# Differential attention on one core: one value product per key tile, or one for each of its two softmax maps

## The chip, the cores and the metric

One core of a Trainium2 chip runs the whole program, a hybrid backbone of two layers. The metric is device time in microseconds (us) of one execution, taken as the median of several. The engines are named as the profile names them: PE is TensorE, PEld its weight loads, DVE is VectorE, ACT is ScalarE, POOL is GpSimd, SP issues DMAs.

## The reference

Each layer normalises 256 context and 1024 latent tokens, projects them, mixes them in three head groups (an RWKV-7 scan in two directions, differential attention, windowed grouped-query attention), projects the result and passes it through a gated MLP. The change touches the differential attention alone. It has four heads; each head has two components m with their own queries and keys of width 32 and a shared value of width 64:

```python
def diff_core(q, k, v, lam):
    s = jnp.einsum('bqhmd,bkhmd->bhmqk', q, k, preferred_element_type=F32) * (DF_QK ** -0.5)
    p = jax.nn.softmax(s, axis=-1)
    p = p[:, :, 0] - lam * p[:, :, 1]
    return jnp.einsum('bhqk,bkhd->bqhd', p.astype(v.dtype), v)
...
    head_out = lambda t: (rms_norm(t, norm_g) * (1.0 - lam_init)).reshape(t.shape[:2] + (DF_W,))
```

Context queries see the 256 context keys, latent queries all 1280 keys.

## The kernel before

Per layer, one stage runs three generators side by side: the RWKV scan (`rw_rest` and what it calls), the differential attention (`df_units`) and the modulation vectors (`ada`). When the scan has ended, the windowed attention (`gq_units`) begins beside the last differential units. A scheduler of the framework, which places instructions by a simulated timeline, decides the order on each engine; dependencies and the buffers of each pool bound it. Every engine then works its own list in order.

A unit of differential attention is one head and one group of query blocks: two context blocks (layer 0 only) or four latent blocks, so 12 units in layer 0 and 8 in layer 1. A unit has two halves, which `streams` interleaves with those of other units:

- `scores` (L1341): for each query block, component and chunk of keys, a score product into a bank `ds` (L1363, L1376), the negated row maximum on DVE (L1365, L1378), and an exponential on ACT that sums its row (L1356). The maxima and sums of the chunks are merged (L1386 to L1392). Then `neg_log` (L1294) works out minus the logarithm of the sum on eight DVE instructions and three ACT exponentials that alternate, L1395 adds it to the row maximum, and `max_rows` (L1214) puts the sum into eight extra rows of the queries, by a product into a bank `od` (L1223) and a DVE product (L1224).
- `values` (L1400): for each tile j of 128 keys, the score product of each component, keys on partitions (L1419, 104 rows, the extra rows among them), and an exponential on ACT (L1420), which thus gives normalised weights. DVE forms p0 + (-lambda) p1 (L1425, `p[:, 0]` of a tile `p`, three buffers). The product with the 128x64 values (L1432) accumulates in 64 of the 128 partitions of the bank `od`: even j in 0 to 63, odd j in 64 to 127. Products are put off by a list `late`, two at a time. After the last one, ACT copies the bank to `doT` (L1409); four products with `fold`, two stacked identities (L1412), add the two halves and turn them to token-major form in a `ds` bank; DVE copies that (L1327), and a root-mean-square norm follows (L1329 to L1334).

There is one `od` bank, and two banks for `ds`, `ada` and the output projection together. All operands of the value product are fp32, and each such product appears in the trace as two passes: 168 products, 336 records. One product uses half of the array's columns.

Of the kernel before, what the change touches and what calls it, by code (L numbers as in the profile page):

```python
# [83 lines left out]
PCP = ()  # L84
# [16 lines left out]
LN2 = math.log(2.0)  # L101
# [56 lines left out]
class K:  # L158
# [1044 lines left out]
    DF_TAGS = ("ks", "qs", "p", "vh", "dy", "dsq", "doT", "mask8d", "fold", "dnm", "dL", "dmn", "dtot", "dnl", "lni", "lne", "dss", "drs", "ms",  # L1203
# [90 lines left out]
    def neg_log(self, y, L, n):  # L1294

        v = self.nc.vector
        it = self.al("lni", [128, 8], 2, I32)[:, :n]
        e = self.al("lne", [128, 8], 2)[:, :n]
        v.tensor_copy(y, L.bitcast(I32))
        v.tensor_scalar(out=y, in0=y, scalar1=-LN2 / (1 << 23), scalar2=LN2 * (127 - 0.043), op0=ALU.mult, op1=ALU.add)  # L1300
        for _ in range(3):
            self.nc.scalar.activation(e, y, AF.Exp)
            v.tensor_tensor(out=e, in0=e, in1=L, op=ALU.mult)
            v.scalar_tensor_tensor(out=y, in0=y, scalar=1.0, in1=e, op0=ALU.add, op1=ALU.subtract)

    def df_units(self, l, late):
# [6 lines left out]
        for hd in range(DF_HEADS):  # L1313
# [11 lines left out]
            def finish(o, t0, nt, hd=hd):  # L1325
                y = self.al("dy", [128, 4, 64], 1)[:, :nt]
                vv.tensor_copy(y, o)  # L1327
# [9 lines left out]
            for gi, (t0, nt) in enumerate(groups):  # L1337
# [3 lines left out]
                def scores(t0=t0, nt=nt, nk=nk, us=us, hs=hs, first=gi == 0, head=head, hd=hd):  # L1341
# [51 lines left out]
                    nl = f(self.al("dnl", [128, 2, nt], 3))  # L1393
                    self.neg_log(nl, tot, 2 * nt)
                    vv.tensor_tensor(out=rows, in0=nl, in1=rows, op=ALU.add)  # L1395
# [4 lines left out]
                def values(t0=t0, nt=nt, nk=nk, us=us, hs=hs, finish=finish):  # L1400
# [4 lines left out]
                    pair = []  # L1405

                    def result():
                        s = self.al("doT", [128, 512], 1)[:, :w]
                        act.activation(s, o[:, :w], AF.Copy)  # L1409
                        u = self.bk(UFB)  # L1410
                        for i in range(nt):
                            mm(u[:, i * 64:i * 64 + 64], s[:, i * 128:i * 128 + 128], self.fold, start=True, stop=True)  # L1412
                        finish(u[:, :nt * 64].rearrange("p (t d) -> p t d", t=nt), t0, nt)

                    for j in range(nk):
# [5 lines left out]
                        if j in PCP:  # L1421
                            gp.tensor_scalar(out=p[:, 1, :w], in0=p[:, 1, :w], scalar1=self.nlam, scalar2=None, op0=ALU.mult)
                            gp.tensor_tensor(out=p[:, 0, :w], in0=p[:, 0, :w], in1=p[:, 1, :w], op=ALU.add)
                        else:
# [877 lines left out]
```

## Time and profile before

| what | before |
|---|---|
| median of 3 runs | 4567.54 us (4542.02 to 4578.57) |
| profiled execution | 4560.47 us, span 4558.6 us |
| PE busy | 4169.8 us (91%) |
| DVE busy | 2917.1 us (64%) |
| ACT busy | 1797.8 us (39%) |
| POOL busy | 2180.7 us (48%) |
| mean granted clock of TensorE | 0.892 |

Busy shares are means over stages with different limits. The differential attention runs from about 430 to 1265 us (layer 0) and from about 2880 to 3640 us (layer 1), and only these stretches hold instructions that the change touches. The chain of waits follows the work that ended last back from the end, so a piece of work on it is time that the end waited for. The granted clock has two levels, 1.0 (2.4 GHz) and 0.5 (1.2 GHz); a fraction is a mean over a stretch.

### The profile page before, as it was taken

The page shows a single profiled execution, that of the slowest core. Times are in us where ns is not written, and L with a number is a line of the kernel's source. Part 1 is how long each engine was busy: PE and PEld are TensorE (multiplying, and loading weights), DVE is VectorE, ACT ScalarE, POOL GpSimd, SP SyncE. Part 2 cuts the span into 40 slices and gives each one's busy share as a digit, 9 for nine tenths or more (in the row PEclk, how much of TensorE's full clock was granted, in tenths as well). Part 3 has the DMA queues.
Part 4 walks back from the last instruction along what each step waited for, and adds up shares of the span by engine and source line. Part 5 has one row for each costly group of instructions (what it writes and reads, how often), then busy time and mean ns, then how long its engine had stood idle before and what let it go on. Part 6 is the DMA issues. An engine that isn't in the chain of part 4 may idle for free.

```text
span 4558.6 us, 67583 instructions
## 1 busy us (share of the span) xinstructions
PE 4169.8 (91%) x24447; PEld 3182.7 (70%) x24447; DVE 2917.1 (64%) x5849; ACT 1797.8 (39%) x3586; POOL 2180.7 (48%) x2151
## 2 busy tenths in 40 slices
PE   8998888898998799979998998888989998999898
PEld 5886655665466699968996786645845466788786
DVE  4346676567665877788777336766677656766443
ACT  3334554544323333343333334555534333333332
POOL 3335324334353666666665425264243445766443
PEclk9997778796899899989998998668988988999999
DMA  6454232234023222232223646132241142222443
GB/s 205 137 135 109 62 85 78 69 95 119 27 68 126 93 84 78 81 116 88 79 84 114 166 115 144 43 80 60 59 121 34 29 133 87 79 83 84 146 149 121
DMA packets 465626, 440.44 MB, mean 97 GB/s; under 512 B 122115, under 2 KB 389515, under 8 KB 465292
## 3 DMA queue, kind: packets, MB, share of 16 engines
q1 hardware_dynamic: 408780, 369.39, 27.4%
q0 software_dynamic: 24352, 62.80, 4.9%
q10 hardware_dynamic: 32160, 3.94, 0.5%
q8 instruction: 193, 3.16, 0.3%
q14 instruction: 141, 1.16, 0.1%
HBM read 340.96 MB, written 95.04 MB: 96 GB/s over the span
## 4 chain that ended last, share of the span: by engine, by line
PE 73%; DVE 13%; DMA 5%; ACT 3%; issue 3%; POOL 2%; SPq 1%; ACTq 0%; DVEq 0%; POOLq 0%
PE m L249 6%; PE m L250 6%; PE m L251 6%; PE b L249 3%; PE b L250 3%; PE od L1432 3%; PE b L251 3%; PE gs L1499 2%; PE gram L955 2%; PE dn L249 2%; PE dn L250 2%; PE dn L251 2%; PE ds L1419 2%; PE gs L1498 2%; PE fm L249 2%
## 5 line engine op out<-in xcount | busy, mean ns | idle before, releaser
L245 POOL TENSOR_TENSOR gp<-gx,gp 128x512 fp32r<-128x512 f32 x160 | 208.4, 1307 | 257.3 <-DVE gp L241 181.9
L239 ACT ACTIVATE fwh<-wraw 128x1024 fp32r<-128x1024 f32 x198 | 206.0, 1055 | 273.0 <-DVE wraw L1849 190.8
L1356 ACT ACTIVATE ds<-ds,dnm 128x512 f32<-128x512 f32 (+1 forms) x400 | 232.4, 581 | 189.2 <-DVE dnm L1378 112.4
L1420 ACT ACTIVATE p<-ds 128x512 f32<-128x512 f32 (+1 forms) x336 | 187.2, 585 | 254.8 <-PE ds L1419 211.8
L245 DVE TENSOR_TENSOR wl<-wraw,fwh 128x1024 fp32r<-128x1024 f32 x110 | 196.8, 1790 | 114.0 <-ACT fwh L239 111.8
L245 POOL TENSOR_TENSOR wl<-wraw,fwh 128x1024 fp32r<-128x1024 f32 x88 | 222.4, 2530 | 95.8 <-ACT fwh L239 95.5
L249 PE MATMUL m<-h,fwh 128*128 128x322 f32 (+1 forms) x660 | 219.8, 333 | 11.0 <-ACT fu L1895 6.8
L1378 DVE TENSOR_REDUCE dnm<-ds 128x1 f32<-128x512 f32 x256 | 173.6, 686 | 84.9 <-PE ds L1376 82.2
L251 PE MATMUL m<-h,wl 128*128 128x322 f32 (+1 forms) x660 | 218.8, 332 | 2.9 <-DVE wl L245 2.9
L245 DVE TENSOR_TENSOR wl<-wr,wh 128x512 fp32r<-128x512 f32 (+1 forms) x76 | 66.6, 878 | 241.8 <-ACT wh L239 128.2
L250 PE MATMUL m<-h,fwh 128*128 128x322 f32 (+1 forms) x660 | 220.1, 334 | 0.0
L245 POOL TENSOR_TENSOR wl<-wr,wh 128x512 fp32r<-128x512 f32 (+1 forms) x76 | 99.8, 1313 | 246.8 <-ACT wh L239 208.1
L1425 DVE SCALAR_TENSOR_TENSOR p<-p,ls 128x512 f32<-128x512 f32 (+1 forms) x168 | 144.8, 863 | 95.3 <-ACT p L1420 93.3
L1432 PE MATMUL od<-p,vh 128*64 128x512 f32 (+1 forms) x336 | 191.0, 707 | 13.4 <-DVE p L1425 9.2
L1376 PE MATMUL ds<-ks,qs 96*128 96x512 f32 x256 | 155.5, 625 | 44.5 <-ACT ds L1356 37.5
L250 PE MATMUL dn<-dl,ahl 128*128 128x512 f32 x440 | 177.5, 403 | 4.4 <-POOL dl L245 4.4
L249 PE MATMUL dn<-dh,ahl 128*128 128x512 f32 x440 | 175.3, 402 | 5.2 <-ACT ahl L239 3.8
L245 POOL TENSOR_TENSOR dl<-dr,dh 128x1024 fp32r<-128x1024 f32 x44 | 109.5, 2489 | 143.2 <-ACT dh L239 143.2
L249 PE MATMUL m<-T,fwh 128*128 128x322 f32 (+1 forms) x436 | 147.1, 338 | 32.7 <-DVE fraw L1866 23.7
L251 PE MATMUL dn<-dh,ahl 128*128 128x512 f32 x440 | 171.4, 399 | 0.0
L1419 PE MATMUL ds<-qs,ks 104*128 104x512 f32 (+1 forms) x336 | 152.7, 496 | 8.8 <-ACT p L1420 5.9
L245 DVE TENSOR_TENSOR dd<-dr,dd 128x1024 fp32r<-128x1024 f32 x44 | 59.0, 1344 | 156.9 <-ACT dd L239 156.9
(572 smaller groups left out, 13490.3 us busy)
## 6 DMA issues: line engine op xcount, KB each, us to landing
dr<-in_ff_w_down_dram SPq DMA_DIRECT2D x88, 512.0 KB
aw<-in_ada_w_dram SPq DMA_DIRECT2D x160, 256.0 KB
wraw<-in_ff_w_gate_dram SPq DMA_DIRECT2D x66, 512.0 KB
wraw<-in_ff_w_up_dram SPq DMA_DIRECT2D x66, 512.0 KB
wr<-in_w_in_dram SPq DMA_DIRECT2D x88, 256.0 KB
x<-scr_x SPq DMA_DIRECT2D x28, 512.0 KB
scr_act<-cv POOLq DMA_DIRECT2D x22, 512.0 KB, 3.0
ar<-scr_act SPq DMA_DIRECT2D x44, 256.0 KB
```

The lines of the kernel that those rows point to most:

```text
L239: nc.scalar.activation(hi, src, AF.Copy)
L245: e.tensor_tensor(out=lo, in0=src, in1=hi, op=ALU.subtract)
L249: mm(out, lh, rh, start=first, stop=False)
L250: mm(out, lh, rl, start=False, stop=False)
L251: mm(out, ll, rh, start=False, stop=last)
L1356: act.activation(s, s, AF.Exp, bias=nm[:, c, m, i:i + 1], accum_out=L[:, c, m, i:i + 1])
L1376: mm(s, us["q"][m][0:96, i * 128:i * 128 + 128], K2[m][0:96, 256 + 512 * c:768 + 512 * c], start=True, stop=True)
L1378: vv.tensor_reduce(out=nm[:, 1 + c, m, i:i + 1], in_=s, axis=AX.X, op=ALU.max, negate=True)
L1419: mm(s[:, :w], hs["K"][m][0:104, j * 128:j * 128 + 128], us["q"][m][0:104, :w], start=True, stop=True)
L1420: act.activation(p[:, m, :w], s[:, :w], AF.Exp)
L1425: vv.scalar_tensor_tensor(out=p[:, 0, :w], in0=p[:, 1, :w], scalar=self.nlam, in1=p[:, 0, :w], op0=ALU.mult, op1=ALU.add)
L1432: mm(o[r:r + 64, :w], v[:, j], p[:, 0, :w], start=j < 2, stop=j >= nk - 2)
```

## The change

The weights of the value product are no longer normalised, and the two components are no longer subtracted before it. For each key tile there are now two products with the same values, one for each component: component 1 into partitions 64 to 127 of `od`, component 0 into 0 to 63, the second queued directly behind the first. After the last tile the bank is transposed whole (four 128x128 transposes in place of the four products with `fold`), and a DVE product multiplies each component by the reciprocal of its sum, times -lambda for component 1; POOL adds the two. `neg_log` and `fold` go, and the extra query rows hold the row maximum alone. A list `late` now takes one tile's two products at a time, and the reciprocals have five buffers. The diff, without lines that only drop names:

```diff
-            def finish(o, t0, nt, hd=hd):
+            def finish(u, r, t0, nt, hd=hd):
+
+                t = self.al("doT", [128, 512], 1)[:, :nt * 128].rearrange("p (b m d) -> p b m d", b=nt, m=2)
+                vv.tensor_tensor(out=t, in0=u, in1=r.rearrange("p (m b) -> p b m", m=2).unsqueeze(3).broadcast_to([128, nt, 2, 64]), op=ALU.mult)
                 y = self.al("dy", [128, 4, 64], 1)[:, :nt]
-                vv.tensor_copy(y, o)
+                gp.tensor_tensor(out=y, in0=t[:, :, 0], in1=t[:, :, 1], op=ALU.add)
...
-                    nl = f(self.al("dnl", [128, 2, nt], 3))
-                    self.neg_log(nl, tot, 2 * nt)
-                    vv.tensor_tensor(out=rows, in0=nl, in1=rows, op=ALU.add)
+                    r = us["r"] = f(self.al("dnl", [128, 2, nt], 5))
+                    vv.reciprocal(out=r, in_=tot)
+                    vv.tensor_scalar(out=r[:, nt:], in0=r[:, nt:], scalar1=self.nlam, scalar2=None, op0=ALU.mult)
...
                         for i in range(nt):
-                            mm(u[:, i * 64:i * 64 + 64], s[:, i * 128:i * 128 + 128], self.fold, start=True, stop=True)
-                        finish(u[:, :nt * 64].rearrange("p (t d) -> p t d", t=nt), t0, nt)
+                            nc.tensor.transpose(u[:, i * 128:i * 128 + 128], s[:, i * 128:i * 128 + 128], self.ident)
+                        finish(u[:, :w].rearrange("p (b m d) -> p b m d", b=nt, m=2), us["r"], t0, nt)
...
-                        if j in PCP:
-                            gp.tensor_scalar(out=p[:, 1, :w], in0=p[:, 1, :w], scalar1=self.nlam, scalar2=None, op0=ALU.mult)
-                            gp.tensor_tensor(out=p[:, 0, :w], in0=p[:, 0, :w], in1=p[:, 1, :w], op=ALU.add)
-                        else:
-                            vv.scalar_tensor_tensor(out=p[:, 0, :w], in0=p[:, 1, :w], scalar=self.nlam, in1=p[:, 0, :w], op0=ALU.mult, op1=ALU.add)
-
-                        pair.append((j, p))
-
-                        def product(pair=tuple(pair)):
-                            for j, p in pair:
-                                r = 64 * (j % 2)
-                                mm(o[r:r + 64, :w], v[:, j], p[:, 0, :w], start=j < 2, stop=j >= nk - 2)
+
+                        def product(j=j, p=p):
+
+
+                            i1 = mm(o[64:128, :w], v[:, j], p[:, 1, :w], start=j == 0, stop=j == nk - 1)
+                            with self.tc.issue_after(i1.ins):
+                                mm(o[0:64, :w], v[:, j], p[:, 0, :w], start=j == 0, stop=j == nk - 1)
                             if j == nk - 1:
                                 result()
 
-                        if j % 2:
-                            late.append(product)
-                            pair.clear()
+                        late.append(product)
                         self.flush(late, DLD[l])
```

Three places in the engines' lists show what moves. The first is PE in layer 0, in the first head's second latent unit: `ds` are score products of successive key tiles, `od` the value products, the rest is RWKV. Before:

```order
L1419 MATMUL ds1697_8410<-qs1569_7863,ks1509_7571 128x512
L1419 MATMUL ds1699_8417<-qs1569_7863,ks1509_7571 128x512
L1432 MATMUL od1669_8295<-p1692_8398,vh1510_7574 64x512
L1419 MATMUL ds1700_8420<-qs1569_7863,ks1509_7571 128x512
L1419 MATMUL ds1702_8425<-qs1569_7863,ks1509_7571 128x512
L814 MATMUL wl1074_5247<-lora551_2775,wa1036_5122 128x256 x2
L1432 MATMUL od1669_8295<-p1695_8406,vh1510_7574 64x512
```

The same unit after the change (L1406 is the score product, L1412 and L1414 the two value products):

```order
L1406 MATMUL ds1694_8382<-qs1564_7836,ks1508_7568 128x512
L1406 MATMUL ds1695_8385<-qs1564_7836,ks1508_7568 128x512
L1412 MATMUL od1663_8258<-p1690_8372,vh1509_7571 64x512
L1414 MATMUL od1663_8258<-p1690_8372,vh1509_7571 64x512
L1406 MATMUL ds1697_8391<-qs1564_7836,ks1508_7568 128x512
L882 MATMUL bon1064_5208<-cols548_2769,bs1063_5205 128x2 x2
L1406 MATMUL ds1698_8394<-qs1564_7836,ks1508_7568 128x512
L1412 MATMUL od1663_8258<-p1693_8381,vh1509_7571 64x512
L1414 MATMUL od1663_8258<-p1693_8381,vh1509_7571 64x512
```

Before, the products of the two column halves mostly stand apart, with score products between them; now the two of a tile stand together, one pair for each tile.

The second place is DVE at the end of that unit's `scores` half (L1391 and L1392 merge the sums, L1378 are the next unit's maxima). Before:

```order
L1391 TENSOR_TENSOR dtot1561_7828<-dL1532_7681 128x8
L1392 TENSOR_TENSOR dtot1561_7828<-dtot1561_7828,dL1532_7681 128x8
L773 SCALAR_TENSOR_TENSOR rk1035_5115<-raw1033_5109,pt97_385,rk1035_5115 128x256
L1299 CAST dnl1562_7836<-dtot1561_7828 128x8
L885 COPY bonus557_2787<-bon910_4380 128x4
L773 SCALAR_TENSOR_TENSOR rk1035_5115<-raw1033_5109,pt97_385,rk1035_5115 128x256
L1300 TENSOR_SCALAR dnl1562_7836<-dnl1562_7836 128x8
L1378 TENSOR_REDUCE dnm1570_7865<-ds1575_7883 128x1
L1378 TENSOR_REDUCE dnm1570_7865<-ds1576_7887 128x1
L1303 TENSOR_TENSOR lne1564_7838<-lne1564_7838,dtot1561_7828 128x8
```

After:

```order
L1381 TENSOR_TENSOR dtot1558_7813<-dtot1558_7813,dL1529_7666 128x8
L771 SCALAR_TENSOR_TENSOR rk1035_5115<-raw1033_5109,pt97_385,rk1035_5115 128x256
L883 COPY bonus557_2787<-bon910_4380 128x4
L1222 TENSOR_TENSOR qs1527_7663<-od1561_7827,mask8d1507_7566 8x512
L1383 RECIPROCAL dnl1559_7821<-dtot1558_7813 128x8
L1367 TENSOR_REDUCE dnm1565_7838<-ds1571_7860 128x1
L1384 TENSOR_SCALAR dnl1559_7821<-dnl1559_7821,ls819_4030 128x4
```

The alternation with ACT is gone, and the extra rows (L1222) are written before the sum's reciprocal instead of after the logarithm.

The third place is PE at the end of the unit. Before:

```order
L1432 MATMUL od1669_8295<-p1714_8493,vh1510_7574 64x512
L1419 MATMUL ds1722_8515<-qs1569_7863,ks1509_7571 128x512
L1432 MATMUL od1669_8295<-p1717_8503,vh1510_7574 64x512
L1432 MATMUL od1669_8295<-p1720_8511,vh1510_7574 64x512
L1412 MATMUL ds1724_8525<-fold1508_7568,doT1723_8523 128x64 x4
```

After:

```order
L826 MATMUL kk1080_5269<-ident_87,rx1079_5267 128x128 x2
L1412 MATMUL od1663_8258<-p1715_8477,vh1509_7571 64x512
L1414 MATMUL od1663_8258<-p1715_8477,vh1509_7571 64x512
L834 MATMUL az1050_5163<-wa1036_5122,lora551_2775 128x256
L1399 MATMUL ds1719_8490<-ident_87,doT1718_8488 128x128 x4
```

Four transposes stand where the four products with `fold` stood.

## Rows read from the trace of the kernel before

**Rows 1.** Page, part 4: shares of the chain that ended last, by engine.

```profile
PE 73%; DVE 13%; DMA 5%; ACT 3%; issue 3%; POOL 2%; SPq 1%; ACTq 0%; DVEq 0%; POOLq 0%
```

**Rows 2.** Busy time by stretch, both stages: us, PE, PEld, DVE, ACT, POOL, PEclk.

```profile
430.00:1265.00 835.00, 749.39 (x5708) 474.49 (x5707) 576.04 (x1471) 397.40 (x980) 322.05 (x480) 0.78 0.28 73
2880.00:3640.00 760.00, 697.33 (x5096) 439.71 (x5096) 519.41 (x1251) 366.20 (x883) 316.78 (x457) 0.83 0.24 62
```

**Rows 3.** The DVE subtraction (page, part 5), and who waited for it (us, times).

```profile
L1425 DVE SCALAR_TENSOR_TENSOR p<-p,ls 128x512 f32<-128x512 f32 (+1 forms) x168 | 144.8, 863 | 95.3 <-ACT p L1420 93.3
...
PEld od L1432: 22.2, 34
PE od L1432: 9.2, 11
```

**Rows 4.** Chain of waits, pieces in both stages: start us, us; first and last each.

```profile
581.26 0.04 DVE p L1425
...
3376.43 0.66 DVE p L1425
...
434.06 0.40 DVE lne L1303
...
3537.73 0.08 DVE dmn L1395
...
552.10 0.59 PE ds L1412 x4
...
3628.42 0.97 PE ds L1412 x8
...
548.73 0.58 PE od L1432 x4
...
3626.59 1.00 PE od L1432 x2
```

**Rows 5.** Timeline of value products: start us, us, and records merged (two a product).

```profile
614.09 1.07 PE L1432 MATMUL od<-p,vh 128*64 128x512 f32 x2 [0.47 <-DVE p L1425]
...
3005.57 1.97 PE L1432 MATMUL od<-p,vh 128*64 128x512 f32 x2
...
3356.98 1.98 PE L1432 MATMUL od<-p,vh 128*64 128x512 f32 x4
...
3034.77 2.63 PE L1432 MATMUL od<-p,vh 128*64 128x512 f32 x4 [2.14 <-DVE p L1425]
3035.43 0.29 PEld L1432 LDWEIGHTS od<-p,vh 128*64 128x64 f32 x2 [0.37 <-DVE p L1425]
```

**Rows 6.** Timeline: four fold products; three 128x128 transposes; then one transpose (min/median/max ns).

```profile
588.22 1.00 PE L1412 MATMUL ds<-fold,doT 128*128 128x64 f32 x8
...
39.54 0.55 PE L493 MATMUL hTp<-ident,x 128*128 128x128 f32 x3
...
L493 PE MATMUL hTp<-ident,x x160: 270/273/476, 39.5 to 2643.2; 128*128 128x128 f32 x160
```

**Rows 7.** Groups by form on DVE: one step of the logarithm, and a reciprocal.

```profile
L1303 DVE TENSOR_TENSOR lne<-lne,dtot 128x8 f32<-128x8 f32 x48 | 11.6, 241 | 8.8 <-ACT lne L1302 8.6
...
L1533 DVE RECIPROCAL ges<-ges 128x4 f32<-128x4 f32 x36 | 6.2, 171 | 0.4
```

**Rows 8.** Lines that answer to the new finish (min/median/max ns; the second from stage 1's groups).

```profile
L1327 DVE COPY dy<-ds x20: 291/424/426, 552.7 to 3629.4; 128x256 f32<-128x256 f32 x16, 128x128 f32<-128x128 f32 x4
...
L957 DVE TENSOR_TENSOR G<-gram,gmask 128x512 f32<-128x512 f32 x40 | 27.5, 690 | 12.1 <-PE gram L955 11.1 <-DMA XT<-scr_i 0.4
...
L1329 POOL TENSOR_TENSOR dsq<-dy x20: 388/612/1062, 553.2 to 3629.9; 128x256 f32<-128x256 f32 x16, 128x128 f32<-128x128 f32 x4
```

**Rows 9.** Busy time by stretch, columns as in rows 2: around one slow stretch of DVE.

```profile
580.00:592.00 12.00, 10.11 (x100) 5.16 (x99) 10.91 (x26) 7.97 (x16) 5.88 (x9) 0.99 0.45 122
592.00:605.50 13.50, 13.50 (x23) 5.07 (x22) 9.02 (x33) 4.88 (x9) 0.42 (x1) 0.50 0.11 30
```

**Rows 10.** Groups of the second stage: the exponentials of `values` and what ended ACT's idle time.

```profile
L1420 ACT ACTIVATE p<-ds 128x512 f32<-128x512 f32 x160 | 90.3, 596 | 106.1 <-PE ds L1419 84.5 <-PE od L1432 20.4
```

More of the change, by code (lines that the diff above doesn't have):

```diff
@@ L83 @@
 RRB = 2
-PCP = ()
 GRAM = 2
@@ L100 @@
 DF_SCALE = 32 ** -0.5
-LN2 = math.log(2.0)
 GQ_SCALE = 64 ** -0.5
@@ L1197, in rw_rest @@
         tg(read((2, 9), end=True))
-    DF_TAGS = ("ks", "qs", "p", "vh", "dy", "dsq", "doT", "mask8d", "fold", "dnm", "dL", "dmn", "dtot", "dnl", "lni", "lne", "dss", "drs", "ms",
+    DF_TAGS = ("ks", "qs", "p", "vh", "dy", "dsq", "doT", "mask8d", "dnm", "dL", "dmn", "dtot", "dnl", "dss", "drs", "ms",
                "aw", "am", "ab")
@@ L1292, in flush @@
             late.pop(0)()
[L1294 to L1304, printed above, removed]
     def df_units(self, l, late):
@@ L1403, in values @@
                     o = self.bk("od")
-                    pair = []
                     def result():
@@ L2202, in run @@
             self.mask8d = self.mask("mask8d", 96)
-            self.fold = self.al("fold", [128, 64])
-            for i in range(2):
-                self.nc.gpsimd.tensor_copy(self.fold[64 * i:64 * i + 64], self.ident[64 * i:64 * i + 64, 64 * i:64 * i + 64])
             ada = self.ada(1, range(8, 24), 4) if last else K.chain(self.ada(0, range(8, 24), 4), self.ada(1, range(8), 4))
```

## The prediction

> **What bounds the kernel now.** I read first the shares of the chain that ended last: PE holds 73% of it and DVE 13% [rows 1], so PE sets the end, and another engine counts only where PE stands waiting for it. Then the two stretches that hold the differential attention, 835 and 760 us: PE is busy for 749.4 and 697.3 us of them, DVE for 576.0 and 519.4 (69% and 68%), ACT for 397.4 and 366.2 [rows 2]. The reader is to see two things. PE is nearly full, yet at a mean granted clock of 0.78 and 0.83: since there are two levels, 44% and 34% of these stretches ran at 1.2 GHz. And DVE is loaded by two thirds but is not the limit as a whole. Third, I read who waits for the subtraction that the change removes: it fills 144.8 us of DVE, but the products behind it waited 22.2 us with their weight loads and 9.2 us in the array [rows 3]. Last, the pieces of the chain of waits inside the two stages, which bound what a removal can give directly: the subtraction stands there in 22 pieces, 18.6 us in all; the logarithm (L1299 to L1304, L1395, its exponentials on ACT) in 55 pieces, 15.3 us; the fold products in 16 pieces, 16.3 us; the value products in 119 pieces, 137.0 us [rows 4], which have the first and the last of each.
>
> **The value products, the term that decides.** The change doubles their number, 168 to 336. A product alone takes 1.07 us at the upper clock and 1.97 us at the lower; the profile shows four records, that is two products for the two column halves, in 1.98 us at the lower clock [rows 5]. So two products that stand together and are both ready cost what one costs. The stretch at 3034.77 shows the same under way: the second product's weight load starts at 3035.43, 0.66 us behind the first product's start, and the four records take 2.63 us, which is 0.66 plus one product of 1.97 [rows 5]. All 168 new pairs stand together in PE's list, wait for the same exponential, and read the same values.
>
> The Trainium skill speaks against it (TensorE: Matmul & The Clock Gate, Part 3, under the mechanism of packing): a weight load overlaps a running product only where their row groups differ, and matmuls start and end strictly in program order. Both products of a pair use all 128 rows, so by that rule the second would follow the first, and each pair would cost two products. The load at 3035.43 lies inside the first product [rows 5], so the trace does not agree; by the rule the sum would be that of the serial rival below, and I take the row.
>
> How many products shared a slot before? In 14 places the timeline merges products of the two halves; 11 of them overlap by their times, the other three have a gap for DVE between them. So before there were 157 slots, and 137.0 / 157 = 0.87 us of chain for each. Now there are 168: **+10 us**. The bounds of one pair are 1.00 slot (the row of 1.98 us) and 2.00 slots.
>
> **What goes from the chain.** The subtraction: **-18.6 us** (from 9.2, where only the array waits, to 31.4, both waits of rows 3). Its 145 us leave DVE too. The logarithm: 9 DVE instructions a unit, of which one step takes 241 ns, and 3 exponentials that alternate with them; in place of them come a reciprocal, 171 ns for the nearest one [rows 7], and one scaling of the same size. Of 15.3 us on the chain I keep two ninths, 3 us: **-12 us**. On DVE as a whole it is 9 x 0.24 x 20 = 43 us less and about 7 us more. The fold: eight records of four products end within 1.00 us; three transposes end within 0.55 us, of which the last takes 0.27 us, so one follows another by 0.14 us, and four take 0.14 x 3 + 0.27 = 0.69 us against 1.00 [rows 6]. The transposes thus save a third of 16.3 us: **-5 us**.
>
> **What is added at a unit's end.** The DVE copy of 128x256 (0.42 us) becomes a product of 128x512 from PSUM, whose nearest row is 0.69 us; POOL's addition is new and nearest to 0.61 us [rows 8]. For 20 units that is 5 us on DVE, 12 us on POOL. It holds a `ds` bank 0.27 us longer; the output that follows only goes to memory, which other heads' units cover. I put **+2 us**; without that cover it would be 17. Below nothing it can't be, since nothing of the old norm goes.
>
> **What is late next.** Where PE waited for the subtraction it now waits for the exponential before it, on which DVE sat idle 93.3 us [rows 3]. That exponential ends earlier than the subtraction by the 0.75 to 0.86 us of the latter, but the pair now stands closer behind its scores. I give back **+5 us** (from 0, where the score products of the next tile cover the exponential, to 17, 0.1 us for each pair).
>
> **The clock.** From 580 to 592 us DVE is busy for 10.9 of 12 us, PE for 10.1; the following 13.5 us ran at a clock of 0.50 with PE busy throughout [rows 9], so they cost about 6.7 us more than at full clock. A subtraction piece of 1.13 us is on the chain inside the first stretch, but RWKV's own DVE work stands beside it there. Pieces of the subtraction lie in about seven such places; all of them cured would give 47 us, none 0. I take **-10 us**, nearer to none, since most low-clock time lies outside the `values` halves.
>
> **Sum.** +10 - 18.6 - 12 - 5 + 2 + 5 - 10 = -28.6 us. Against the profiled execution (4560.5 us, which is 7 us below the median of the runs) that is 4532 us, and on the median's scale 4539 us. What a reordered list changes beyond these terms is in no row; I leave it at nothing, with both sides in the range. **4539 us**, 0.6% below the median.
>
> **The rivals.**
> - *The freed DVE lifts the whole stage.* DVE loses 145 + 36 - 5 = 176 us net of 1095 [rows 2], 16%. If the RWKV work behind it moves up and low-clock time shrinks with it by a fifth (about 625 us of the two stages are low, each worth half of itself), another 62 us go, less the 10 taken: 4487 us. For it: DVE stands at two thirds busy in both stages. Against it: only 18.6 us of the chain were the subtraction's, and the long stretches without any subtraction also ran at low clock.
> - *The pair runs one behind the other* (the change doesn't do what it says). Then each pair costs two slots: 168 x 0.87 = 146 us more, 4685 us. If only the passes follow in order, each half alone, it is about half of a slot, 73 us, 4612 us. The rows at 3356.98 and 3034.77 speak against both; they are few, and component 1's half now comes first.
> - *The exponential takes the subtraction's place as the wait.* This ends on the slower side. The pair waits for component 1's exponential, issued last, 0.596 us long [rows 10]. If ACT, which now has only itself between score and product, is late by as much as half of one for each of the 168 pairs, that is 50 us in place of the 5 taken: 4584 us; with one low-clock stretch more per unit of layer 1 it is over 1% slower. It decides from about 0.2 us of wait a pair on. For it: ACT also serves the scan and the other units' scores. Against it: in `values`, ACT's own idle time ended with score products, 84.5 of 106.1 us in layer 1 [rows 10]; it is PE that is late.
>
> **How the numbers follow.** The forecast, direct terms with little of the clock, has 0.56 and its own range is 4505 to 4565 us. The freed DVE has 0.24 (4440 to 4520). The new wait has 0.14 (4565 to 4625), the serial pair 0.06 (4600 to 4700). 1% of the median is 46 us, about what a measurement of this kernel can tell from no change, so faster means under 4522 and slower over 4613. The forecast gives 0.11 to faster (its bounds 31.4 for the wait and 47 for the clock together) and the rest to the same; the freed DVE goes wholly to faster; the new wait gives 0.04 to slower, the serial pair 0.06. That is faster 0.35, same 0.55, slower 0.10. The range 4475 to 4595 leaves out the lower part of the freed DVE (0.08), the upper part of the new wait (0.05) and the serial pair (0.06).
>
> **What would show it.** Right: pairs of four records in about 1.07 us at full clock and 1.98 at the lower, their total on the chain near 147 us; DVE about 176 us less busy in the two stages; waits of the product now for the exponential, under 20 us; transposes of a unit within 0.7 us. The prediction is wrong if the second product of a pair starts only when the first ends, if the granted clock of the two stages moves by more than 0.03 either way, or if the product's wait for ACT exceeds the 31.4 us that it had for DVE.

## The result: 1.1% slower, and the profile after

The changed kernel takes 4601.81 us (median of 10 runs, 4581.88 to 4624.87); the kernel before, beside it, 4557.14 us (10 runs, 4540.69 to 4578.57). The ratio is 1.0109, 95% interval [1.0085, 1.0133]. The forecast was 4539 us with a range up to 4595, so the time lies outside it, on the slower side. The profiled execution of the changed kernel is the slowest of its ten (4624.87 us) and that of the kernel before a middling one (4560.47). Of the 64 us between the two profiles 44 are the distance of the means, so clocks that are read from these two profiles overstate the loss; a faster execution of the same lists stands at e3, below.

Page of the changed kernel: engines' busy time and shares of the chain; then the lines of the score product, the exponential and the two value products of `values`.

```profile
PE 4236.6 (92%) x24711; PEld 3235.3 (70%) x24711; DVE 2783.0 (60%) x5541; ACT 1794.6 (39%) x3526; POOL 2173.1 (47%) x2167
PE 73%; DVE 12%; DMA 6%; ACT 3%; issue 2%; POOL 2%; SPq 1%; ACTq 0%; POOLq 0%; DVEq 0%
L1407 ACT ACTIVATE p<-ds 128x512 f32<-128x512 f32 (+1 forms) x336 | 188.5, 585 | 270.4 <-PE ds L1406 260.2
L1412 PE MATMUL od<-p,vh 128*64 128x512 f32 (+1 forms) x336 | 197.5, 676 | 0.0
L1414 PE MATMUL od<-p,vh 128*64 128x512 f32 (+1 forms) x336 | 197.5, 676 | 0.0
L1406 PE MATMUL ds<-qs,ks 104*128 104x512 f32 (+1 forms) x336 | 153.3, 496 | 10.8 <-ACT p L1407 7.2
```

The same two stretches as in [rows 2], of the changed kernel (us, PE, PEld, DVE, ACT, POOL, PEclk, DMA share, GB/s):

```profile
430.00:1265.00 835.00, 758.84 (x5787) 484.91 (x5786) 484.76 (x1268) 394.07 (x942) 313.88 (x486) 0.75 0.28 73
2880.00:3640.00 760.00, 695.34 (x5017) 452.81 (x5018) 420.61 (x1045) 351.10 (x838) 283.10 (x439) 0.75 0.24 60
```

DVE is freed, by 134 us over the whole span (2783.0 against 2917.1) where 176 were forecast. In the two stretches it is 905 us against 1095, but they are fixed in time and the changed kernel runs later, so some of its work has left them. And the granted clock fell from 0.78 to 0.75 and from 0.83 to 0.75 [rows 2]. The loss sits in the part of each stage in which the scan runs, from its first Gram product to its last. Of the kernel before:

```profile
429.00:989.00 560.00, 498.26 (x4536) 335.63 (x4535) 379.61 (x959) 289.09 (x725) 207.29 (x347) 0.78 0.27 70
2852.00:3321.00 469.00, 423.49 (x3840) 295.62 (x3840) 321.56 (x724) 258.62 (x646) 189.35 (x316) 0.79 0.24 60
```

and of the changed kernel:

```profile
433.00:1021.00 588.00, 531.74 (x4714) 357.03 (x4714) 332.87 (x846) 291.42 (x700) 207.77 (x357) 0.74 0.26 70
2861.00:3404.00 543.00, 502.36 (x4028) 347.84 (x4027) 292.79 (x689) 269.39 (x652) 192.53 (x328) 0.70 0.21 55
```

The second scan part is 74 us longer and the first 28; the rest of the span is 38 us shorter, in part since more of the attention's work now stands inside the scan parts (x4028 records against x3840 in the second). In the second, PE idles less than before (40.6 us against 45.5). Length times clock hardly differs there: 371 us before and 380 us after. **This product, a length counted at the full clock, is the measure that the rest of this document uses.** For the whole span, as a mean of runs, it is 4064.4 us before (25 runs, span 4557.7, clock 0.8918) and 4057.8 us after (10 runs, span 4601.8, clock 0.8818). So at full clock the changed kernel is 6.6 us shorter, worth 7.4 us at the old clock. The 0.010 of clock cost 4057.8 x (1/0.8818 - 1/0.8918) = 51.6 us. The sum, +44.2, is the measured difference of the spans, 44.1. (A wait at the low clock counts half in it too, so it is a measure of the split and not of PE's work alone.)

One place, in layer 1, where the scan's block goes its own way. The changed kernel (columns as above):

```profile
3188.00:3224.00 36.00, 33.67 (x242) 11.00 (x238) 5.83 (x23) 19.52 (x36) 29.45 (x50) 0.99 0.27 75
3224.00:3229.60 5.60, 0.93 (x7) 0.50 (x5) 0.69 (x1) 0.60 (x1) 4.96 (x9) 1.00 1.14 223
3229.60:3250.00 20.40, 16.28 (x130) 11.15 (x130) 10.25 (x29) 13.43 (x35) 3.33 (x6) 0.50 0.51 140
3250.00:3270.00 20.00, 20.00 (x138) 16.98 (x137) 6.88 (x11) 6.62 (x18) 2.67 (x5) 0.50 0.05 11
3270.00:3290.00 20.00, 20.00 (x136) 16.51 (x135) 9.89 (x23) 7.54 (x19) 2.63 (x5) 0.50 0.06 11
3290.00:3304.70 14.70, 14.70 (x155) 12.07 (x154) 6.49 (x14) 2.24 (x7) 1.50 (x4) 0.50 0.21 60
```

The kernel before, over the same work:

```profile
3190.00:3200.00 10.00, 9.90 (x67) 5.09 (x66) 3.04 (x5) 6.07 (x13) 3.53 (x4) 1.00 0.31 62
3200.00:3220.00 20.00, 20.00 (x293) 16.73 (x293) 13.56 (x35) 6.83 (x19) 6.91 (x13) 1.00 0.64 137
3220.00:3240.00 20.00, 20.00 (x231) 17.01 (x231) 12.72 (x21) 11.96 (x31) 4.52 (x9) 1.00 0.13 25
```

What stands between, in the chain of waits of the changed kernel:

```profile
3221.54 0.68 PE ds L1406 x2
3222.22 0.29 issue
3222.50 6.91 DMA ks<-scr_df
3229.41 0.14 issue
3229.55 0.68 PE ds L1352 x2
...
3239.74 2.36 DMA XT<-scr_i
```

The reader is to see three things. The value and score products stood packed for 36 us at the full clock, with no scan work among them. Then PE had 0.93 us of work in 5.6, since the next head's keys (`ks`, one buffer) are loaded only when the last head is done with them. Then the clock was 0.50 for 75 us, although PE was busy without a break for the last 54.7 of them; the kernel before did a like mix of scan and scores, as densely, at 1.00. A low clock that lasts does not look like waiting: it looks like a busy PE.

### The profile page after: what moved, and what is told of

Same layout as the page of the kernel before. It is cut to its first block, busy times and chain, and to the rows that moved or that the text cites. A ratio compares the mean times of both kernels' runs of the same rounds, so it can differ in the third digit from the quotient of the medians.

```text
span 4622.8 us, 67684 instructions
## 1 busy us (share of the span) xinstructions
PE 4236.6 (92%) x24711; PEld 3235.3 (70%) x24711; DVE 2783.0 (60%) x5541; ACT 1794.6 (39%) x3526; POOL 2173.1 (47%) x2167
## 4 chain that ended last, share of the span: by engine, by line
PE 73%; DVE 12%; DMA 6%; ACT 3%; issue 2%; POOL 2%; SPq 1%; ACTq 0%; POOLq 0%; DVEq 0%
PE m L247 6%; PE m L248 6%; PE m L249 6%; PE od L1412 3%; PE b L247 3%; PE b L249 3%; PE b L248 3%; PE gram L953 2%; PE ds L1406 2%; PE gs L1479 2%; PE dn L247 2%; PE dn L248 2%; PE dn L249 2%; PE ds L1365 2%; PE gs L1478 2%
## 5 line engine op out<-in xcount | busy, mean ns | idle before, releaser
L1365 PE MATMUL ds<-ks,qs 96*128 96x512 f32 x256 | 165.2, 667 | 55.4 <-ACT ds L1345 44.5
L1412 PE MATMUL od<-p,vh 128*64 128x512 f32 (+1 forms) x336 | 197.5, 676 | 0.0
L1414 PE MATMUL od<-p,vh 128*64 128x512 f32 (+1 forms) x336 | 197.5, 676 | 0.0
L1406 PE MATMUL ds<-qs,ks 104*128 104x512 f32 (+1 forms) x336 | 153.3, 496 | 10.8 <-ACT p L1407 7.2
```

The source lines that it names most:

```text
L1365: mm(s, us["q"][m][0:96, i * 128:i * 128 + 128], K2[m][0:96, 256 + 512 * c:768 + 512 * c], start=True, stop=True)
L1406: mm(s[:, :w], hs["K"][m][0:104, j * 128:j * 128 + 128], us["q"][m][0:104, :w], start=True, stop=True)
L1412: i1 = mm(o[64:128, :w], v[:, j], p[:, 1, :w], start=j == 0, stop=j == nk - 1)
L1414: mm(o[0:64, :w], v[:, j], p[:, 0, :w], start=j == 0, stop=j == nk - 1)
```

## Experiments

Four theories were on the table first. **A**: the change altered the order of PE's list, and with it the granted clock. **B**: the new pair of products itself lowers the clock. **C**: the freed DVE lets value products pack into a block of their own, PE runs dry behind it, and the scan then stands at the low clock. Their rival throughout is **W**: time follows the work and the waits on the path.

**e1_pairs_only**: the kernel before with the pairs alone. The logarithm, the normalised weights and `fold` stay; -lambda moves into the lower half of `fold`, so the subtraction goes.

```diff
-                            vv.scalar_tensor_tensor(out=p[:, 0, :w], in0=p[:, 1, :w], scalar=self.nlam, in1=p[:, 0, :w], op0=ALU.mult, op1=ALU.add)
...
+                            i1 = mm(o[64:128, :w], v[:, j], p[:, 1, :w], start=j == 0, stop=j == nk - 1)
+                            with self.tc.issue_after(i1.ins):
+                                mm(o[0:64, :w], v[:, j], p[:, 0, :w], start=j == 0, stop=j == nk - 1)
```

> The kernel before with the value products of the change alone: two per key tile, queued as a pair, the DVE subtraction gone; the logarithm, the normalised weights and the fold stay (minus lambda goes into the lower half of the fold matrix). Theory A (the loss is the granted clock, which follows from where each engine's list puts scan work and value work; PE's work at full clock hardly changes): a new list, so anywhere from -30 to +50 us against before, with span times mean clock within 15 us of before's 4069 us. Theory B (a pair of fp32 products, which fills both column halves, itself brings the clock down): +30 to +50 us, as the whole change, and the granted clock low inside the stretches of pairs. Theory C (DVE freed of the subtraction lets the value products pack into one block, PE runs dry at its end, and the scan block behind it runs at the lower clock): +30 to +50 us, low clock in the scan blocks and not inside the pairs.

Measured: 4547.81 us, ratio 0.9968 [0.9938, 0.9997], mean clock 0.895, full-clock length 4068.0 us. The pairs and the freed DVE are both in it, and it is not slower but the fastest of the three. B falls at the size that it asked for (30 to 50 us), and C as far as it blames the subtraction's removal. The 36 us at 0.99 above, packed with pairs, speak against B too. A smaller effect of the pairs is not excluded, since this is one order of the list (see e9 to e12).

**e2_no_log**: the kernel before without the logarithm; it leaves out the normalisation by the sums.

```diff
-                    nl = f(self.al("dnl", [128, 2, nt], 3))
-                    self.neg_log(nl, tot, 2 * nt)
-                    vv.tensor_tensor(out=rows, in0=nl, in1=rows, op=ALU.add)
```

> The kernel before without the logarithm of the sums: the weights are not normalised and the subtraction, the products and the fold stay, so the normalisation by the sums is left out. Theory A: a new list, anywhere from -40 to +40 us, span times clock within 20 us of 4069. Theory B: 15 to 25 us faster than before (the logarithm's 12 us on the chain and its 40 us of DVE), clock as before, since no pair is formed. Theory C: 0 to 20 us faster, since most of DVE's load (the subtraction, 145 us) stays.

Measured (4 runs): 4647.29 us, ratio 1.0186 [1.0135, 1.0237], clock 0.8765, full-clock length 4067.3. Nothing but work was taken out, and the kernel became 1.9% slower than before, and slower than the changed one. W falls: with the full-clock length about where it was, no wait or term of work explains it.

**e3_free_order**: the changed kernel without the rule that holds the second product behind the first.

```diff
-                            with self.tc.issue_after(i1.ins):
-                                mm(o[0:64, :w], v[:, j], p[:, 0, :w], start=j == 0, stop=j == nk - 1)
+                            mm(o[0:64, :w], v[:, j], p[:, 0, :w], start=j == 0, stop=j == nk - 1)
```

> The changed kernel without the rule that the second product of a pair must follow the first in PE's list. Theory A: another list, -40 to +30 us against the changed kernel (-0 to +75 against before is 4557 to 4630). Theory B: pairs that come apart no longer fill both halves, so the clock rises by 0.005 or more; time falls only if the added slots cost less than that. Theory C: as the changed kernel within 15 us, since DVE's load is the same.

Measured: 4589.83 us, ratio 1.0063 [1.0039, 1.0087], clock 0.8846, length 4061.2. The edit changes nothing that runs: in the trace DVE, ACT and POOL work the same lists as in the changed kernel, and PE's 24711 records come in the same order, but for two that change places with a neighbour. So it says nothing of the rule. It is a second set of ten runs of the changed kernel, with a mean span of 4591.1 us against 4601.8. Two sets of one program thus lie 0.2% apart, and the loss is 1.1% by the one and 0.6% by the other, at the edge of what their intervals allow.

Its profiled execution is its fastest, where the changed kernel's was the slowest. The two scan parts, the wait for `ks` and the low stretch of the head that was shown above, and the 425 records that ran there at 0.50 from 3250.0 to 3304.7 us (columns as above, the wait as in the chain of waits):

```profile
426.00:1008.00 582.00, 528.17 (x4714) 358.30 (x4713) 332.81 (x846) 291.03 (x700) 207.70 (x357) 0.75 0.26 70
2838.00:3357.00 519.00, 475.30 (x4056) 325.28 (x4044) 291.63 (x691) 269.28 (x652) 194.10 (x329) 0.75 0.22 58
...
3194.85 7.00 DMA ks<-scr_df
3199.60:3230.30 30.70, 24.18 (x189) 18.10 (x189) 14.45 (x36) 15.23 (x41) 5.37 (x12) 0.50 0.45 112
3222.70:3257.30 34.60, 34.41 (x425) 29.03 (x424) 22.28 (x46) 16.00 (x44) 6.56 (x12) 0.89 0.15 38
```

The same wait stands there, and the clock falls before it is over, as it fell right behind it at 3229.6 us. But the low stretch ends after 30.7 us instead of 75, and the same records in the same order take 34.6 us at 0.89 instead of 54.7 at 0.50. **One list does not have one clock: it differs from execution to execution, and clocks of single profiles must be read with that in mind.**

**e4_dve_load_back**: the changed kernel with the subtraction's DVE time put back, into a tile that nobody reads.

```diff
+                        x = self.al("px", [128, 512], 1, BF16)
+                        vv.scalar_tensor_tensor(out=x[:, :w], in0=p[:, 1, :w], scalar=self.nlam, in1=p[:, 0, :w], op0=ALU.mult, op1=ALU.add)
```

> The changed kernel with DVE's load put back: the old subtraction runs for each key tile into a scratch tile that nothing reads. Theory A: a new list, -40 to +40 us against the changed kernel, no sign forecast. Theory B: 0 to +25 us against the changed kernel, the pairs being the same. Theory C: 25 to 45 us faster than the changed kernel, back near the kernel before, because the value block is stretched again and the scan's products fill it.

Measured (4 runs): 4619.04 us, ratio 1.0109 [1.0046, 1.0171], clock 0.8802, length 4063.9. DVE is busy again for 2908.7 us, and no clock comes back; with e1, C falls, as far as one order of each can tell.

All three lists without the logarithm (the changed kernel's, e2's and e4's) lost clock and the one with it gained some. So a theory **D** came up: the logarithm's wait had held the score and value blocks back, and kept scan work among them. Against it **R**: any new order of the list moves the clock, either way, and the logarithm has no part in it.

**e5_log_wait**: the changed kernel, whose extra rows again wait for a logarithm that enters with a factor of zero.

```diff
+                    nl = f(self.al("dlg", [128, 2, nt], 3))
+                    self.neg_log(nl, tot, 2 * nt)
+                    vv.scalar_tensor_tensor(out=rows, in0=nl, scalar=0.0, in1=rows, op0=ALU.mult, op1=ALU.add)
```

> The changed kernel with the logarithm put back as a wait alone: the old code for it runs on VectorE and ScalarE, and its result enters the exponents' row with a factor of zero, so that the row waits for it as before; normalisation and pairs stay as changed. Theory D (the logarithm's wait held the attention's rows back, so that the scan's small products did not stand in blocks of their own; without it the blocks lie where the low clock is granted): the time goes back to that of e1_pairs_only, ratio to the kernel before 0.994 to 1.003, and the granted clock of the second layer's scan stretch (first to last gram product) from 0.70 back to 0.78 or more. Theory R (any new order of TensorE's list moves the clock by chance, the logarithm has no part in it): the ratio can fall anywhere between 0.995 and 1.02, and the two scan stretches need not move together. Theory W (the time follows the work on the path): the logarithm's 12 us in the fill of the stage come back, 4602 + 12 = 4614, ratio 1.013, with the clock as in the changed kernel.

Measured: 4579.08 us, ratio 1.0055 [1.0015, 1.0094], clock 0.886, length 4059.9. The two scan parts of its profiled execution, the second slowest of its ten (4610.9 us):

```profile
425.00:1011.00 586.00, 534.71 (x4625) 366.17 (x4625) 343.46 (x925) 288.24 (x718) 207.71 (x360) 0.72 0.26 69
2859.00:3378.00 519.00, 469.10 (x3983) 330.18 (x3983) 301.63 (x743) 266.14 (x660) 188.37 (x324) 0.73 0.22 57
```

D wanted 0.78 in the second and has 0.73; W wanted 1.013 and the interval leaves that out. Work was added, and the time is 0.5% below the changed kernel's first set of runs, but only 0.1% below the second (e3), and not at e1's level. This fits R and decides little alone. Its ten runs say one thing more: the same program took from 4561.28 us (clock 0.891) to 4614.17 us (clock 0.881), with a full-clock length that varied by 5.5 us (standard deviation) around 4059.9.

**e6_fill_steps** and **e7_before_fill_steps**: both kernels with 72 dummy products of 128x512, written into a bank that is overwritten next.

```diff
         po = self.bk("y")
+        for i in range(2):
+            mm(po, self.ident, kv[:, :, 256:512], start=True, stop=True)
```

> The changed kernel with pure extra work on TensorE: in every step of the scan that forms an output, two dummy 128x512 fp32 products go into the bank that the step's own output products then overwrite (72 in all). At 1.07 us each at the full clock that is 77 us more, at the low clock 2 us each and 154 us more. Theory A (what is lost is the granted clock in stretches in which TensorE is busy with small products): the large products raise the clock of the two scan stretches from 0.74 and 0.70 to 0.80 or more, and the time lies between 60 us less and 40 us more than the changed kernel's (ratio to the kernel before 0.996 to 1.019). Theory W (time follows work and waits): 77 to 154 us more than the changed kernel, ratio 1.028 to 1.045, clock unchanged.

> The kernel before with the same 72 dummy products as e6_fill_steps. Theory A: its scan stretches run at 0.78 and 0.79 already, so the filler has less to give back; the clock goes to 0.83 or more, the time to between 10 us less and 60 us more (ratio 0.998 to 1.013), and the distance to e6_fill_steps shrinks from 1.1% to under 0.6%. Theory W: 77 to 154 us more, ratio 1.017 to 1.034, and the distance to e6_fill_steps stays at 1.1%.

Measured (4 runs each): e6 4607.81 us, ratio 1.0131 [1.0079, 1.0184], clock 0.8988, length 4139.2; e7 4609.03 us, ratio 1.0132 [1.0080, 1.0183], clock 0.8978, length 4134.8. The scan parts of e6:

```profile
429.00:1019.00 590.00, 536.89 (x4874) 346.32 (x4875) 341.30 (x863) 295.18 (x711) 213.52 (x364) 0.82 0.28 74
2842.00:3383.00 541.00, 501.51 (x4073) 334.50 (x4066) 294.80 (x691) 267.13 (x648) 194.54 (x329) 0.76 0.22 56
```

In the changed kernel 81 us more of full-clock length cost 4 us of span (4605.5 against 4601.8; against e3's 4591.1 it is 14), since the clock of the scan parts rose from 0.74 to 0.82 and from 0.70 to 0.76 (in e3's execution they stood at 0.75; A had asked for 0.80 in both). In the kernel before, 70 us more cost 48, and its clock rose less than A had it (0.81 and 0.78 in the scan parts). The distance between the two kernels, 1.1%, went to nothing. W falls with e6, and the mean clocks of the two are the highest of all the kernels here (0.8988 and 0.8978). But the dummies also bring a new order of the list, and what that alone does to the clock isn't separated from what the filler does.

**e8_fill_heads**: six such products ahead of each head's first scores, where PE waits for `ks`.

```diff
+                        s = self.bk("ds")
+                        for _ in range(6):
+                            mm(s, self.ident, self.ident.unsqueeze(1).broadcast_to([128, 4, 128]), start=True, stop=True)
                         head()
```

> The changed kernel with six dummy 128x512 fp32 products ahead of the first scores of each of the eight heads, where TensorE waits for the new head's keys (31.8 us of such waits in the second layer, 4 of them): 48 products, 51 us at the full clock, of which the waits can hide 6 us at a head. Theory G (the clock falls in the gap at a head's start, and what follows runs at the low clock for long): the low stretches that begin there shorten, above all the 75 us at 3229.6 us of the second layer, the clock of the second scan stretch rises from 0.70 to 0.78 or more, and the time is 20 to 80 us under the changed kernel's (ratio 0.994 to 1.007). Against it: the low stretches are as long as before though the gaps are filled, and the time is equal or up to 60 us more (ratio 1.011 to 1.024).

Measured: 4583.91 us, ratio 1.0073 [1.0044, 1.0102], clock 0.8934, length 4094.6 (+37). The head that was shown above, and the second scan part:

```profile
3193.32 5.32 PE L1334 MATMUL ds<-ident 128*128 128x512 f32 x12
...
3204.10:3231.50 27.40, 26.82 (x183) 22.13 (x184) 9.53 (x15) 11.44 (x31) 2.91 (x6) 0.50 0.14 29
2857.00:3350.00 493.00, 454.49 (x4021) 311.46 (x4021) 289.93 (x681) 266.38 (x648) 192.96 (x328) 0.80 0.24 61
```

The low stretch behind this head is 27.4 us long instead of 75, and the second scan part stands at 0.80 instead of 0.70, as G had it. But without any filler e3's execution of the changed lists has 30.7 us and 0.75 in these places, and the list of e8 is another one too: dummies left out, 5% of its triples of successive PE records are not in the changed kernel's, as against 6% in e9 and 4% in e11, which alter the order alone. The mean span is 19 us below the changed kernel's and 8 below e3's, with 48 products more in it; the ratio of 1.0073 lies just above what G gave, and its interval overlaps that of the changed kernel and that of e3. So e8 fits G and does not show it; R explains as much. What the traces do show is that the clock fell in the wait for `ks` or right behind it in both executions of the changed lists. (The 31.8 us of waits that were expected for layer 1 are those of both layers; layer 1 has 24.2, in 2 waits.)

**e9 to e12**: no instruction is added or removed; one planning number is altered in both kernels, so that the lists stand in other orders. Against R stands **S**: the changed kernel is at a lower clock whatever the order, since the old waits are gone.

```diff
-AHD = (0.3, 0.3)
+AHD = (0.2, 0.2)
...
-HPO = (4000, 1000)
+HPO = (3000, 1000)
```

> The changed kernel with one number of the order's planner altered: the attention units' lead over the scan is 0.2 for 0.3 in both layers. No instruction is added or removed; TensorE's list only stands in another order. Theory R (the full-speed length of the span stays at 4058, and the order of the list alone moves the granted clock, in either direction): span times mean clock 4050 to 4072, time anywhere from 0.995 to 1.02 of the kernel before, following the clock. Theory S (without the logarithm's and the subtraction's waits this kernel is at a lower clock whatever the order): ratio 1.006 to 1.016 again, clock 0.878 to 0.886.

> The kernel before with the same number at 0.2. Theory R: the order it was tuned for is one of many, and another order loses clock like the change did: span times mean clock 4055 to 4075, ratio 1.003 to 1.02, clock below 0.888. Theory S: the old waits keep its clock up in any order: ratio 0.997 to 1.004, clock 0.889 to 0.894.

> The changed kernel with another number altered: the priority of the attention units in the first layer 3000 for 4000. Again no instruction more or less. Theory R: span times mean clock 4050 to 4072, ratio anywhere from 0.995 to 1.02. Theory S: 1.006 to 1.016.

> The kernel before with the same priority of 3000. Theory R: ratio 1.003 to 1.02 with a clock below 0.888. Theory S: 0.997 to 1.004.

Measured, as ratios to the kernel before as it stands (10 runs each, e10 4):

| order | before | changed |
|---|---|---|
| as given | 1 (clock 0.892) | 1.0109 [1.0085, 1.0133], 0.882 |
| lead 0.2 | 1.0162 [1.0106, 1.0218], 0.879 | 1.0013 [0.9980, 1.0046], 0.893 |
| priority 3000 | 1.0073 [1.0047, 1.0098], 0.888 | 1.0034 [1.0009, 1.0058], 0.887 |

The scan parts of layer 1, with lead 0.2, first of the changed kernel:

```profile
2826.00:3332.00 506.00, 458.92 (x4022) 312.84 (x4021) 290.81 (x686) 269.57 (x651) 190.60 (x326) 0.77 0.22 57
```

and of the kernel before:

```profile
2883.00:3367.00 484.00, 445.27 (x3749) 305.39 (x3750) 303.27 (x683) 243.97 (x597) 185.85 (x315) 0.75 0.22 55
```

S falls: with lead 0.2 the changed kernel is the faster one by 1.5% (1.0013/1.0162). R holds in the main: an order alone moves either kernel by 0.7 to 1.6%, in mean spans by 28 us (changed, priority 3000; 17 against e3's runs) to 75 us (before, lead 0.2), where two sets of one program lay 11 us apart. The full-clock lengths are 4074.4 and 4058.6 for the changed kernel and 4070.7 and 4077.8 for the one before; the first lies just above the 4072 that R had given, and the clock of e12, 0.8883, just above its 0.888.

Changed against before, order by order, the time differs by +1.1, -1.5 and -0.4% and the full-clock length by -6.6, +3.7 and -19.2 us (a mean of 4063.6 against 4071.0). **So three orders do not show that the change itself makes the kernel faster or slower; the measured +1.1% belongs to the two orders that were compared.** The order as given is the best of the three for the kernel before and the worst for the changed one. If it was picked for the kernel before, as e10's expectation says, that is no accident; no run here tests it. The fastest of all kernels, e1, stands under the same reserve: its full-clock length of 4068 is no shorter than before, it has the better clock.

What stays open: by which property of a list one could tell its clock ahead. Nor does a list have one clock, as e3 shows. Dry spells at a head may be part of it, which e8 leaves open, and so may the logarithm's wait, which e5 leaves open.

## Why the prediction was wrong, step by step

- **The pair: right.** In the changed kernel's timeline (start us, us) the second product starts 0.01 us behind the first, and a whole pair ends 1.08 us after its start at the full clock, and 1.98 us at the low one:

```profile
3220.46 0.64 PE L1412 MATMUL od<-p,vh 128*64 128x512 f32 x1
3220.47 0.64 PE L1414 MATMUL od<-p,vh 128*64 128x512 f32 x1
...
3220.94 0.59 PE L1412 MATMUL od<-p,vh 128*64 128x512 f32 x1
3220.95 0.59 PE L1414 MATMUL od<-p,vh 128*64 128x512 f32 x1
...
557.79 1.12 PE L1412 MATMUL od<-p,vh 128*64 128x512 f32 x1
557.80 1.12 PE L1414 MATMUL od<-p,vh 128*64 128x512 f32 x1
...
558.70 1.06 PE L1412 MATMUL od<-p,vh 128*64 128x512 f32 x1
558.71 1.06 PE L1414 MATMUL od<-p,vh 128*64 128x512 f32 x1
```

  On the chain the value products now hold 149 us (261 pieces of L1412, the first and the last below, and as many of L1414 of 0.01 us), against 137.0 before [rows 4] and 147 forecast; in e3's execution of the same lists, at a higher clock, it is 139, so that the total is that near is in part the low clock. The serial rival is dead. The Trainium skill (TensorE: Matmul & The Clock Gate, Part 3, mechanism of packing) lets a weight load overlap a running product only where their row groups differ. Both products here use all rows, and the second product's second load starts at 3220.52 us, inside both running first passes, so the trace does not agree. The prediction also took the Trainium skill too narrowly there: the same Part measures a speed-up for products side by side in column groups. The pair, 1.08 us where one product took 1.07, agrees with that.

```profile
3220.52 0.14 PEld L1414 LDWEIGHTS od<-p,vh 128*64 128x64 f32 x1
...
547.30 0.62 PE od L1412
...
3671.17 0.42 PE od L1412
```

- **The subtraction, -18.6: right in kind, its size not measured.** It is off the chain, and what took its place is small: the product waited 2.4 us, 4 times, for its exponential, far below the 20 that I gave as a bound; the score products waited 7.2 us for one, against 5.9 before. The rival of the exponential is dead too, though the measured time falls into its range: a time does not prove a mechanism. What the term was worth by itself no run tells: e1, which trades the subtraction for the pairs, has a full-clock length of 4068.0 us, no shorter than before.

```profile
  ACT p L1407: 2.4, 4
```

- **The fold and the finish: right in kind.** Four transposes take 0.66 us where four fold products took 1.00 [rows 6], the DVE product 692 ns and POOL's addition 724 ns, near the 0.69 and 0.61 us of [rows 8]:

```profile
3224.98 0.66 PE L1399 MATMUL ds<-ident,doT 128*128 128x128 f32 x4 [0.76 <-ACT doT L1396]
...
L1314 DVE TENSOR_TENSOR doT<-ds,dnl x20: 424/692/693, 554.4 to 3675.7; 128x512 f32<-128x512 f32 x16, 128x256 f32<-128x256 f32 x4
L1316 POOL TENSOR_TENSOR dy<-doT x20: 452/724/835, 554.9 to 3676.5; 128x256 f32<-128x256 f32 x16, 128x128 f32<-128x128 f32 x4
```

- **The direct sum, -18.6 without the clock: not borne out at its size.** The full-clock length fell by 6.6 us (by 3.2 in e3's runs of the same program), a third or less of the sum, and over three orders it moved by -6.6, +3.7 and -19.2, so that even the sign is not settled. The logarithm's -12 was counted as pure gain, and e2, which removes it alone, has a full-clock length of 4067.3, no shorter than before. Why the pieces were worth so little, whether PE's own work closes up behind them or the new order takes it back, no run tells.
- **The clock, -10: this is the step that failed.** It measured about +52 us (44 with the runs of e3 counted in). I read [rows 9] as a busy DVE that starves PE, behind which the clock falls, and let less DVE work give clock back. e4 puts that load back and no clock comes with it. The rival of the freed DVE made the same error with a larger sum. The low clock in the scan parts moves with the order of the lists (e9 to e12), and from execution to execution (e3). The sum had called what a reordered list changes "in no row" and left it "at nothing", and it was worth more than all the other terms together: kernels with little or no change of work spread from 0.9968 to 1.0186. The prediction's own sign of failure, a clock that moves by more than 0.03, did come in the profiled execution (0.83 to 0.75); in e3's the same stretch has 0.80.
- **The range** ended at 4595 because slower was tied to mechanisms on the path. Its slower side had to hold what another order costs by itself, which for the kernel before is +0.7% and +1.6% (e12, e10).

## What to carry to other kernels

Where PE is busy nine tenths of the time and still spends a fifth of its time at the low clock (a mean of 0.892), multiply span by mean clock for every run: if that product stays and the time moves, the change is in the clock and not in the work. Then rerun both versions in a few harmless other orders before believing a difference of 1 or 2%; three still left about half a per cent open here, the standard error of the distance of the two means. An edit that leaves every list as it was is a repeat: compare the lists first, and read from it what a repeat differs by (0.2% here). A range for such a kernel must hold the spread of orders on both sides, whatever the sum of the terms says.

## What the runs showed of the hardware

- PE that is busy without a break can stay at the low clock: 54.7 us from 3250.0 to 3304.7, and in layer 0 the changed kernel's two stretches

```profile
529.70:560.40 30.70, 30.70 (x266) 22.47 (x265) 9.38 (x33) 8.79 (x23) 5.87 (x13) 0.50 0.23 57
563.80:591.10 27.30, 27.30 (x218) 15.59 (x216) 3.80 (x9) 6.55 (x13) 2.02 (x4) 0.50 0.19 52
```

  where the kernel before ran a like mix, with fewer value products, at 1.00:

```profile
520.20:550.00 29.80, 29.80 (x434) 24.07 (x434) 20.40 (x51) 15.94 (x44) 7.91 (x17) 1.00 0.31 75
```

  The Trainium skill (TensorE: Matmul & The Clock Gate, Part 1) gives the full clock to an array that has been kept busy, and takes it away in gaps. The second half agrees with the head at 3224 us; the first does not hold in these rows, where the records say busy and the clock stayed low. (The ends of matmuls are modelled in these records, so busy need not mean a full array.)
- The same instructions in the same order can run at either level: 425 records took 54.7 us at 0.50 in one execution and 34.6 us at 0.89 in another (e3).
- Extra matrix work can cost almost nothing: 81 us of it at full clock added 4 to 14 us to the changed kernel, and with 37 us of it that kernel was 8 to 19 us shorter. Removing work can cost: the logarithm alone, gone, +1.9%. Each of these came with a new order of the list, whose part is not separated.
